# The second half of the tokens enters the up projection without its norm; the 1/rms is multiplied onto its gate and value rows

## The chip, the cores and the metric

The kernel runs on one core of a Trainium2 chip. The metric is the device time of one execution in microseconds (us). Five engines work side by side, each on its own queue of instructions in order: TensorE (PE, matrix products; its weight loads are shown as PEld), VectorE (DVE), ScalarE (ACT), GpSimd (POOL) and SyncE (SP), whose queue issues the DMA transfers here.

## The reference

One step of a hybrid decoder layer for 1024 prompt tokens and 8 single tokens of a second group, 1032 in all, in fp32. The part that matters:

```python
def rmsnorm(x, w):
    xf = x.astype(jnp.float32)
    y = xf * lax.rsqrt(jnp.mean(xf * xf, axis=-1, keepdims=True) + EPS)
    return (y * w.astype(jnp.float32)).astype(x.dtype)
...
    x = x + jnp.concatenate([o_a, y], axis=-1) @ w['w_out']

    h = rmsnorm(x, w['norm2_w'])
    gate, val = jnp.split(h @ w['w_up'], 2, axis=-1)
    gate, buf_f_new = causal_dwconv(gate, buf_f, w['ffn_conv_w'], w['ffn_conv_b'])
    x = x + (jax.nn.silu(gate) * val) @ w['w_down']
```

Ahead of it stand the input projection, a gated linear recurrence and a state-space mixer (the two that `o_a` and `y` come from), behind it a final norm. The model width is 1024, the MLP width 2816. The norm's factor 1/rms is one number for each token, so it may be multiplied onto h's inputs or onto the rows of gate and value that come out.

## The kernel before

Tokens run along the free axis, channels along the 128 partitions. An fp32 product is built from three matmuls on numbers split into a high part (`wh`, `uh`, an ACT cast) and a low part (`wl`, `ul`, a DVE subtraction): high by high, high by low, low by high.

**Out projection** (`out_job`, L1015 to L1046). Its last jobs, o4.0.hf to o4.6.hf, finish the residual rows `xh[hf][m]` (shown as x) of one half hf of the tokens: a product of 12 matmuls into a bank `mm`, then DVE adds it to x (L1040, the eviction). `final` (L1048) then sends the row to DRAM (`x1_d`), squares it on ACT (L1055, `n2sq`) and adds the square to the running sum `n2r` on POOL (L1056; the tensor is `rst` in the code).

**Norm** (`set_norm`, L1111). For a quarter of the tokens (258) PE multiplies `n2r` by a matrix of ones into a bank `n2ms`, which sums over the channels; `rstd_of` (L635) makes 1/rms of it: ACT L637, then DVE L638 to L640. The bank has the tag "nx", of which there is one (`NBANK = {"mx": 4, "nx": 1}`, L37). The first of the DVE operations, L638, still reads the bank.

**Operands of the up projection** (`set_of(i)`, L1120). The 1032 tokens form two instances, i = 0 and 1, of 516 tokens each. Of each instance's rows, four blocks are made (two halves of the channels by two quarters of the tokens), and the 2x2 block product is computed in seven products (p1 to p7) in place of eight. `norm` multiplies x by the norm's weight and by 1/rms on DVE (L1133, 8 operations an instance); `comb` makes the sums of blocks `sm` (L1151, DVE or POOL); `put` splits an operand into `uh` (ACT L1143) and `ul` (DVE L1144).

**Weights.** There are 22 weight tiles j. `up_load(j)` fetches gate and value columns (`ws`) and makes four sums of weight blocks on POOL (L1208, `wt`); `up_split(j, n)` splits two products' weights at a time (ACT L1227, DVE L1228).

**Products** (`Up`, L1236 to L1285). A product has 12 matmuls. p1, p7 and p3 go to one of three banks (`ua`), the others to one of four (`ub`). Each is evicted by the method of its name: p1 and p5 by ACT copies, p6 L1254, p7 L1262 (with two POOL subtractions L1263 and L1264), p2 L1270, p4 L1278 to L1282 and p3 L1285 by DVE. The rows of the gate go to `fext`, those of the value to `val`; `last` holds the last ten gate tokens. `up_close` runs the width-3 convolution (DVE L334 among it) and SiLU, multiplies (L1301) and stores.

**Order of the work.** PE's order is the program's own (L1317 to L1334); one `tick` is one matmul, `after(n, work)` runs a piece of code n ticks later, `spread(pieces, n)` one piece every n ticks. The other engines' instructions are ordered by a scheduler on top of that. At weight tile 0 all seven products of instance 0 come first and then all of instance 1 (`FIRST`); from tile 1 on the two instances alternate (`ORDER`). Instance 0's operands are made while the out projection of the second half still runs; instance 1's while PE works through instance 0 at tile 0. After the 22 tiles the down projection follows (`down`, bank `dn`, evicted by DVE L1387, weights split at L184 of `wload`).

Of the kernel before, what the change touches and what calls it, by code (L numbers as in the profile page):

```python
# [12 lines left out]
ALU = mybir.AluOpType  # L13
# [5 lines left out]
T = 1024  # L19
# [31 lines left out]
def hybrid_layer(  # L51
# [963 lines left out]
    def out_job(r0, m, halves=(0, 1), last=False):  # L1015
        def load():
            w = wload(w_out[0, r0 * P:(r0 + 4) * P, m * P:(m + 2) * P], 4, 2 * P)
            return w, [residual_load(m + i) for i in range(2)] if r0 == 8 else None

        def run(loads):  # L1020
            w, res = loads
            if r0 not in mixes:
                mixes[r0] = mix_load(r0)
            hi, lo = mixes[r0]
            if res:
                for hf in range(2):
                    xpair[hf][m // 2] = tl("big", "x1")[:, :NT].rearrange("p (i t) -> p i t", i=2)
                    for i in range(2):
                        xh[hf][m + i] = xpair[hf][m // 2][:, i, :]
            for i in range(2):  # L1030
                for hf in halves:
                    for c in range(2):
                        cs, ts_ = slice(c * QW, (c + 1) * QW), slice((2 * hf + c) * QW, (2 * hf + c + 1) * QW)
                        ps = psmm.tile([P, 512], F32, tag="mm", name=nm("mm"))[:, :QW]
                        yield from steps(w, i * P, (i + 1) * P, hi, lo, ts_, ps)
                        x_ = xh[hf][m + i][:, cs]
                        if res:
                            A.copy(x_, ps)
                        else:
                            V.tensor_tensor(x_, x_, ps, op=ALU.add)  # L1040
                        if last:
                            final(m + i, x_, ts_)
                        yield True
                if res:
                    spread(residual([xh[hf][m + i] for hf in range(2)], *res[i]), 8)
        job(f"o{r0}.{m}" + (f".{halves[0]}" if len(halves) == 1 else ""), load, run)  # L1046

    def final(m, x_, ts_):  # L1048

        SP.dma_start(x1_d[m][:, ts_], x_)  # L1050
        if m == 0:
            A.activation(rst[:, ts_], x_, AF.Square)
        else:
            sq = tl("us", "n2sq")
            A.activation(sq, x_, AF.Square)  # L1055
            G.tensor_tensor(rst[:, ts_], rst[:, ts_], sq, op=ALU.add)  # L1056

    xpair = [[None] * 4 for _ in range(2)]

# [59 lines left out]

    def set_of(i):  # L1120

        ts_ = slice(2 * i * QW, 2 * (i + 1) * QW)
        xp = [t.rearrange("p i (c t) -> p i c t", c=2) for t in xpair[i]]

# [30 lines left out]
            return [t[:, 0:2], t[:, 2:4]]  # L1155

        s_ = []
        yield from norm(0)
        if i:
            yield from put("p1", a1, "hT")  # L1160
        yield from norm(1)
        yield from put("p2", a2, "big")
        if i == 0:
            yield from put("p4", b2, "e")
        yield from comb(s_, V, b1, b2, ALU.subtract)
        yield from comb(s_, V, two(s_[0]), a1, ALU.subtract)
        yield from comb(s_, G, a1, b1, ALU.subtract)
        yield from comb(s_, G, two(s_[1]), a2, ALU.add)
        if i == 0:
            while "o0.6.1" not in done:  # L1170
                yield
            yield from put("p1", a1, "hT")
        else:
            yield from put("p4", b2, "big")
        yield from put("p6", [s_[1]], "hT")
        if i == 0:
            up_load(0)
        yield from put("p5", [s_[0]], "hT")
        if i == 0:
            up_split(0, 0)  # L1180
            yield
        yield from put("p7", [s_[2]], "hT")
        if i == 0:
            up_split(0, 1)
            yield
        yield from put("p3", [s_[3]], "big")

    ORDER = ("p1", "p6", "p5", "p7", "p2", "p4", "p3")

# [41 lines left out]
    class Up:  # L1231
# [40 lines left out]
        def p4(self, ps):  # L1272
# [4 lines left out]
            n = e - c.start  # L1277
            V.tensor_tensor(self.ext[:, 2 + c.start:2 + e], self.u3[:, :n], ps[:, :n], op=ALU.add)  # L1278
            if n < QW:
                dreg = self.ext[:, 2 + T:2 + T + 24].rearrange("p (b r) -> p b r", r=3)  # L1280
                V.tensor_tensor(dreg[:, :, 2:3], self.u3[:, n:].unsqueeze(2), ps[:, n:].unsqueeze(2), op=ALU.add)
                V.tensor_tensor(last10[:, self.j, :], self.u3[:, QW - 10:], ps[:, QW - 10:], op=ALU.add)  # L1282

        def p3(self, ps):
            V.tensor_tensor(self.val[:, self.at(0)], self.u2, ps, op=ALU.add)  # L1285

    def up_open(j):
        ext, val = tl("x5", "fext"), tl("x5", "val")
# [15 lines left out]
    def ups(j, seq):  # L1304

        us_ = up_open(j)
        for n, (name, i) in enumerate(seq):
            yield from us_[i].mul(name)
            if n == 2 and j + 1 < FT:
                up_load(j + 1)  # L1310
            if n in (5, 9, 13) and j + 1 < FT:
                up_split(j + 1, (5, 9, 13).index(n))
            if n == 1 and j:
                up_split(j, 3)
        up_close(j, us_[0])
# [1 line left out]
    with tc.manual_schedule(engines={mybir.EngineType.PE}):  # L1317
# [6 lines left out]
            tick()  # L1324
        up_split(0, 2)
        up_split(0, 3)
        after(20, lambda: set_norm(1, 0))
        after(29, lambda: set_norm(1, 1))
        after(33, lambda: spread(set_of(1), 2))
        for _ in ups(0, [(name, i) for i in range(2) for name in FIRST]):  # L1330
            tick()
        for j in range(1, FT):
# [124 lines left out]
```

## Time and profile before

| | us |
|---|---|
| median of 3 runs (lowest to highest) | 1781.82 (1781.15 to 1788.02) |
| the profiled execution | 1782.61 |
| its span, first to last instruction | 1780.9 |
| busy: PE, DVE, ACT, POOL | 1725.4, 1119.3, 817.5, 405.3 |
| granted TensorE clock, mean | 0.991 |

A row of a timeline reads: start, length, engine, line, operation, output<-inputs, shapes, how often in a row; in brackets how long the engine had been idle before it and which instruction released it. A row of windows gives the stretch, its length, then the busy time of PE, PEld, DVE, ACT and POOL in it with the number of instructions, the granted clock, the busy share of the DMA engines and GB/s. Matmul lengths overlap, so PE's pace is read from the distance of starts, or from the busy time of a stretch over its matmuls.

### The profile page before, as it was taken

The page shows a single profiled execution, that of the slowest core. Times are in us where ns is not written, and L with a number is a line of the kernel's source. Part 1 is how long each engine was busy: PE and PEld are TensorE (multiplying, and loading weights), DVE is VectorE, ACT ScalarE, POOL GpSimd, SP SyncE. Part 2 cuts the span into 40 slices and gives each one's busy share as a digit, 9 for nine tenths or more (in the row PEclk, how much of TensorE's full clock was granted, in tenths as well). Part 3 has the DMA queues.
Part 4 walks back from the last instruction along what each step waited for, and adds up shares of the span by engine and source line. Part 5 has one row for each costly group of instructions (what it writes and reads, how often), then busy time and mean ns, then how long its engine had stood idle before and what let it go on. Part 6 is the DMA issues. An engine that isn't in the chain of part 4 may idle for free. (4 is left out here: it accounts for less than half of the span.)

```text
span 1780.9 us, 38506 instructions
## 1 busy us (share of the span) xinstructions
PE 1725.4 (97%) x16143; PEld 1675.6 (94%) x16143; DVE 1119.3 (63%) x2011; ACT 817.5 (46%) x1464; POOL 405.3 (23%) x415
## 2 busy tenths in 40 slices
PE   7999899999999999999999978999999999999998
PEld 6998799999999999999899978999999999999997
DVE  6667966575564565458645768666666666445545
ACT  7677688455554454545333435334333344111114
POOL 2113331220110111011000364554445542000001
PEclk9999999999999999999999998999999999999999
DMA  4144634642221222234334432222222225422212
GB/s 154 39 126 126 189 106 132 184 137 98 87 66 51 86 73 78 58 109 155 101 108 133 135 90 72 72 72 78 82 91 72 72 84 203 152 81 90 97 61 96
DMA packets 218019, 182.34 MB, mean 102 GB/s; under 512 B 13388, under 2 KB 195158, under 8 KB 217830
## 3 DMA queue, kind: packets, MB, share of 16 engines
q1 hardware_dynamic: 217558, 179.80, 32.3%
q8 instruction: 126, 2.06, 0.5%
q14 instruction: 47, 0.39, 0.1%
q0 software_dynamic: 288, 0.10, 0.0%
HBM read 141.53 MB, written 38.52 MB: 101 GB/s over the span
## 5 line engine op out<-in xcount | busy, mean ns | idle before, releaser
L93 PE MATMUL mm<-hh,wh 128*128 128x344 f32 x1248 | 405.3, 325 | 0.3 <-issue 0.2
L93 PE MATMUL mm<-hl,wh 128*128 128x344 f32 x1248 | 404.5, 324 | 0.0
L93 PE MATMUL mm<-hh,wl 128*128 128x344 f32 x1248 | 402.0, 322 | 0.0
L93 PEld LDWEIGHTS mm<-hh,wh 128*128 128x128 f32 x1248 | 235.0, 189 | 3.9 <-issue 2.6
L93 PEld LDWEIGHTS mm<-hl,wh 128*128 128x128 f32 x1248 | 235.2, 189 | 2.4 <-issue 0.9
L93 PEld LDWEIGHTS mm<-hh,wl 128*128 128x128 f32 x1248 | 235.3, 189 | 2.2 <-issue 1.5
L183 ACT CAST wh<-ws 128x1024 fp32r<-128x1024 f32 x96 | 100.5, 1047 | 242.8 <-PE dn L93 135.3
L93 PE MATMUL ub<-ul,wh 128*128 128x258 f32 x704 | 200.4, 285 | 4.3 <-DVE ul L1144 4.3
L93 PE MATMUL ub<-uh,wh 128*128 128x258 f32 x704 | 200.3, 285 | 2.0 <-ACT uh L1143 2.0
L93 PE MATMUL ub<-uh,wl 128*128 128x258 f32 x704 | 200.2, 284 | 0.0
L93 PE MATMUL dn<-ah,wh 128*128 128x256 f32 (+1 forms) x640 | 181.1, 283 | 1.2 <-DVE x L1387 1.2
L93 PE MATMUL dn<-al,wh 128*128 128x256 f32 (+1 forms) x640 | 180.6, 282 | 0.0
L93 PE MATMUL dn<-ah,wl 128*128 128x256 f32 (+1 forms) x640 | 180.2, 282 | 0.0
L184 DVE TENSOR_TENSOR wl<-ws,wh 128x1024 fp32r<-128x1024 f32 x96 | 126.4, 1317 | 72.4 <-ACT wh L183 71.4
L93 PE MATMUL mm<-mh,wh 128*128 128x258 f32 x512 | 147.7, 288 | 11.2 <-DVE x L1040 8.3
L93 PE MATMUL ua<-ul,wh 128*128 128x258 f32 x528 | 149.4, 283 | 0.9 <-DVE ul L1144 0.9
L93 PE MATMUL ua<-uh,wh 128*128 128x258 f32 x528 | 149.2, 283 | 0.0
L93 PE MATMUL ua<-uh,wl 128*128 128x258 f32 x528 | 148.4, 281 | 0.0
L93 PE MATMUL mm<-ml,wh 128*128 128x258 f32 x512 | 145.8, 285 | 0.7 <-DVE ml L999 0.7
L93 PE MATMUL mm<-mh,wl 128*128 128x258 f32 x512 | 145.9, 285 | 0.0
L93 PEld LDWEIGHTS ub<-ul,wh 128*128 128x128 f32 x704 | 134.5, 191 | 5.0 <-DVE ul L1144 5.0
L93 PEld LDWEIGHTS ub<-uh,wh 128*128 128x128 f32 x704 | 134.0, 190 | 2.5 <-ACT uh L1143 2.5
(347 smaller groups left out, 3942.8 us busy)
## 6 DMA issues: line engine op xcount, KB each, us to landing
ws<-in_w_in_dram SPq DMA_DIRECT2D x52, 512.0 KB
ws<-in_w_up_dram SPq DMA_DIRECT2D x44, 512.0 KB
ws<-in_w_out_dram SPq DMA_DIRECT2D x24, 512.0 KB
act_d<-val SPq DMA_DIRECT2D x22, 516.0 KB
al<-act_d SPq DMA_DIRECT2D x22, 516.0 KB
ws<-in_w_down_dram SPq DMA_DIRECT2D x22, 512.0 KB
ml<-mix_d SPq DMA_DIRECT2D x48, 172.0 KB
csb<-cs_d SPq DMA_DIRECT2D x32, 256.0 KB
```

What stands on the lines that cost most here:

```text
L93: PE.matmul(out, lhsT, rhs, start=start, stop=stop)
L183: A.copy(wh[:, :n], ws[:, :n])
L184: V.tensor_tensor(wl[:, :n], ws[:, :n], wh[:, :n].bitcast(F32), op=ALU.subtract)
```

## The change

Instance 1 is no longer normed before its products. `weigh(m)` multiplies a row by the norm's weight alone, on ACT, 28 matmuls after the row's last product of the out projection; the eight operations L1133 of instance 1 are gone. `set_of(1)` starts 4 ticks into tile 0, was 33, and advances every 4 ticks, was 2. Both token sums of instance 1 stand together at tick 93, that is 9 matmuls into instance 1's first product; they were at ticks 20 and 29. For each weight tile, 1/rms is multiplied onto the gate rows of instance 1 (DVE, 128x508 and 128x8, after p4) and onto its value rows (POOL, 128x516, after p3); `last` becomes two small POOL copies. The weights of tile 0 are split later (the second piece 76 ticks after the first), and those of tile 1 are loaded and split later within tile 0.

```diff
@@ -1040,6 +1040,8 @@
                             V.tensor_tensor(x_, x_, ps, op=ALU.add)
                         if last:
                             final(m + i, x_, ts_)
+                            if hf and c:
+                                after(28, lambda m=m + i: weigh(m))
                         yield True
                 if res:
                     spread(residual([xh[hf][m + i] for hf in range(2)], *res[i]), 8)
@@ -1054,6 +1056,13 @@
             sq = tl("us", "n2sq")
             A.activation(sq, x_, AF.Square)
             G.tensor_tensor(rst[:, ts_], rst[:, ts_], sq, op=ALU.add)
+
+    weighed = set()
+
+    def weigh(m):
+
+        A.activation(xh[1][m], xh[1][m], AF.Copy, scale=col("n2", m))
+        weighed.add(m)
 
     xpair = [[None] * 4 for _ in range(2)]
 
@@ -1119,6 +1128,7 @@
 
     def set_of(i):
 
+
         ts_ = slice(2 * i * QW, 2 * (i + 1) * QW)
         xp = [t.rearrange("p i (c t) -> p i c t", c=2) for t in xpair[i]]
 
@@ -1155,35 +1165,40 @@
             return [t[:, 0:2], t[:, 2:4]]
 
         s_ = []
-        yield from norm(0)
-        if i:
-            yield from put("p1", a1, "hT")
-        yield from norm(1)
-        yield from put("p2", a2, "big")
         if i == 0:
+            yield from norm(0)
+            yield from norm(1)
+            yield from put("p2", a2, "big")
             yield from put("p4", b2, "e")
-        yield from comb(s_, V, b1, b2, ALU.subtract)
-        yield from comb(s_, V, two(s_[0]), a1, ALU.subtract)
-        yield from comb(s_, G, a1, b1, ALU.subtract)
-        yield from comb(s_, G, two(s_[1]), a2, ALU.add)
-        if i == 0:
+            yield from comb(s_, V, b1, b2, ALU.subtract)
+            yield from comb(s_, V, two(s_[0]), a1, ALU.subtract)
+            yield from comb(s_, G, a1, b1, ALU.subtract)
+            yield from comb(s_, G, two(s_[1]), a2, ALU.add)
             while "o0.6.1" not in done:
                 yield
             yield from put("p1", a1, "hT")
+            yield from put("p6", [s_[1]], "hT")
+            up_load(0)
+            yield from put("p5", [s_[0]], "hT")
+            yield from put("p7", [s_[2]], "hT")
+            yield from put("p3", [s_[3]], "big")
+            up_split(0, 0)
+            after(76, lambda: up_split(0, 1))
         else:
+            d_ = []
+            yield from comb(d_, G, a1, b1, ALU.subtract)
+            yield from put("p1", a1, "hT")
+            while len(weighed) < KT:
+                yield
+            yield from put("p2", a2, "big")
+            yield from comb(s_, V, b1, b2, ALU.subtract)
+            yield from comb(s_, V, two(s_[0]), a1, ALU.subtract)
+            yield from comb(s_, G, two(s_[1]), a2, ALU.add)
             yield from put("p4", b2, "big")
-        yield from put("p6", [s_[1]], "hT")
-        if i == 0:
-            up_load(0)
-        yield from put("p5", [s_[0]], "hT")
-        if i == 0:
-            up_split(0, 0)
-            yield
-        yield from put("p7", [s_[2]], "hT")
-        if i == 0:
-            up_split(0, 1)
-            yield
-        yield from put("p3", [s_[3]], "big")
+            yield from put("p6", [s_[1]], "hT")
+            yield from put("p5", [s_[0]], "hT")
+            yield from put("p7", d_, "hT")
+            yield from put("p3", [s_[2]], "big")
 
     ORDER = ("p1", "p6", "p5", "p7", "p2", "p4", "p3")
 
@@ -1277,12 +1292,20 @@
             n = e - c.start
             V.tensor_tensor(self.ext[:, 2 + c.start:2 + e], self.u3[:, :n], ps[:, :n], op=ALU.add)
             if n < QW:
-                dreg = self.ext[:, 2 + T:2 + T + 24].rearrange("p (b r) -> p b r", r=3)
-                V.tensor_tensor(dreg[:, :, 2:3], self.u3[:, n:].unsqueeze(2), ps[:, n:].unsqueeze(2), op=ALU.add)
-                V.tensor_tensor(last10[:, self.j, :], self.u3[:, QW - 10:], ps[:, QW - 10:], op=ALU.add)
+
+                ext, t0 = self.ext, self.at(0).start
+                dnew = ext[:, 2 + T:2 + T + 24].rearrange("p (b r) -> p b r", r=3)[:, :, 2:3]
+                V.tensor_tensor(dnew, self.u3[:, n:].unsqueeze(2), ps[:, n:].unsqueeze(2), op=ALU.add)
+                V.tensor_tensor(ext[:, 2 + t0:2 + T], ext[:, 2 + t0:2 + T], rst[:, t0:T], op=ALU.mult)
+                V.tensor_tensor(dnew, dnew, rst[:, T:NT].unsqueeze(2), op=ALU.mult)
+                G.tensor_copy(last10[:, self.j, 0:2], ext[:, T:T + 2])
+                G.tensor_copy(last10[:, self.j, 2:10].unsqueeze(2), dnew)
 
         def p3(self, ps):
             V.tensor_tensor(self.val[:, self.at(0)], self.u2, ps, op=ALU.add)
+            if self.i:
+                t0 = self.at(0).start
+                G.tensor_tensor(self.val[:, t0:NT], self.val[:, t0:NT], rst[:, t0:NT], op=ALU.mult)
 
     def up_open(j):
         ext, val = tl("x5", "fext"), tl("x5", "val")
@@ -1306,10 +1329,11 @@
         us_ = up_open(j)
         for n, (name, i) in enumerate(seq):
             yield from us_[i].mul(name)
-            if n == 2 and j + 1 < FT:
+            if n == (2 if j else 5) and j + 1 < FT:
                 up_load(j + 1)
-            if n in (5, 9, 13) and j + 1 < FT:
-                up_split(j + 1, (5, 9, 13).index(n))
+            at_ = (5, 9, 13) if j else (9, 11, 13)
+            if n in at_ and j + 1 < FT:
+                up_split(j + 1, at_.index(n))
             if n == 1 and j:
                 up_split(j, 3)
         up_close(j, us_[0])
@@ -1324,9 +1348,8 @@
             tick()
         up_split(0, 2)
         up_split(0, 3)
-        after(20, lambda: set_norm(1, 0))
-        after(29, lambda: set_norm(1, 1))
-        after(33, lambda: spread(set_of(1), 2))
+        after(4, lambda: spread(set_of(1), 4))
+        after(93, lambda: (set_norm(1, 0), set_norm(1, 1)))
         for _ in ups(0, [(name, i) for i in range(2) for name in FIRST]):
             tick()
         for j in range(1, FT):
```

Three places show how the instructions stand now. (Line numbers of the changed kernel are higher: L1144 became L1154, L1151 L1161, L1228 L1243, L1254 L1269, L1262 L1277, L1270 L1285, L1278 L1293, L1285 L1305.)

PE at the token sums `n2ms` of instance 1, before: the first stands inside p2 of instance 0 (`ub_1488`), the second in p4 (`ub_1491`), ten matmuls later.

```order
L93 MATMUL ub_1488_12430<-ul_1404_11922,wh_1446_12166 128x258
L93 MATMUL n2ms_1489_12439<-n2r_125_804,ones_550 128x258
L93 MATMUL ub_1488_12430<-uh_1403_11921,wl_1447_12167 128x258
L93 MATMUL ub_1488_12430<-uh_1403_11921,wh_1446_12166 128x258
L93 MATMUL ub_1488_12430<-ul_1404_11922,wh_1446_12166 128x258
L93 MATMUL ub_1488_12430<-uh_1403_11921,wl_1447_12167 128x258
L93 MATMUL ub_1491_12451<-uh_1407_11949,wh_1453_12205 128x258
L93 MATMUL ub_1491_12451<-ul_1408_11950,wh_1453_12205 128x258
L93 MATMUL ub_1491_12451<-uh_1407_11949,wl_1454_12206 128x258
L93 MATMUL ub_1491_12451<-uh_1407_11949,wh_1453_12205 128x258
L93 MATMUL ub_1491_12451<-ul_1408_11950,wh_1453_12205 128x258
L93 MATMUL n2ms_1492_12457<-n2r_125_804,ones_550 128x258
```

The same of the changed kernel: both stand next to each other inside p1 of instance 1 (`ua_1521`).

```order
L93 MATMUL ua_1521_12585<-uh_1488_12438,wh_1453_12204 128x258
L93 MATMUL ua_1521_12585<-ul_1489_12439,wh_1453_12204 128x258
L93 MATMUL ua_1521_12585<-uh_1488_12438,wl_1454_12205 128x258
L93 MATMUL n2ms_1522_12595<-n2r_125_804,ones_550 128x258
L93 MATMUL n2ms_1524_12602<-n2r_125_804,ones_550 128x258
L93 MATMUL ua_1521_12585<-uh_1488_12438,wh_1453_12204 128x258
L93 MATMUL ua_1521_12585<-ul_1489_12439,wh_1453_12204 128x258
L93 MATMUL ua_1521_12585<-uh_1488_12438,wl_1454_12205 128x258
```

The two sums share one bank, and between them there was a product's worth of other matmuls; now there is none.

DVE around the operations that read these sums, before: `nt_1490` (L638, reads the first sum) stands right behind the last weight split of tile 0 (`wl_1483`) and ahead of instance 1's norm (L1133).

```order
L1228 TENSOR_TENSOR wl_1483_12408<-ws_1434_12132,wh_1482_12407 128x512
L638 SCALAR_TENSOR_TENSOR nt_1490_12441<-n2ms_1489_12439,n2r_125_804 128x258
L1270 TENSOR_TENSOR fext_1484_12411<-us_1487_12428,ub_1488_12430 128x258
L639 SCALAR_TENSOR_TENSOR nt_1490_12441<-nt_1490_12441,n2r_125_804 128x258
L640 SCALAR_TENSOR_TENSOR n2r_125_804<-nt_1490_12441,n2r_125_804 128x258
L638 SCALAR_TENSOR_TENSOR nt_1493_12459<-n2ms_1492_12457,n2r_125_804 128x258
L639 SCALAR_TENSOR_TENSOR nt_1493_12459<-nt_1493_12459,n2r_125_804 128x258
L640 SCALAR_TENSOR_TENSOR n2r_125_804<-nt_1493_12459,n2r_125_804 128x258
L1133 SCALAR_TENSOR_TENSOR x1_1129_9594<-x1_1129_9594,vcol_99,n2r_125_804 128x516 x2
L1133 SCALAR_TENSOR_TENSOR x1_1151_9891<-x1_1151_9891,vcol_99,n2r_125_804 128x516 x2
```

DVE of the changed kernel, the rows ahead of `nt_1523`, which reads the first sum: instance 1's sums (`sm`), low parts (`ul`) and the evictions of instance 0's products. Ahead of these rows, from the last eviction of the out projection on, stand `wl_1483`, `ul_1489`, `fext_1484` (of p2), `sm_1495` and `ul_1494`, one instruction each.

```order
L1161 TENSOR_TENSOR sm_1497_12492<-sm_1495_12480,x1_1151_9891 128x516
L1269 TENSOR_TENSOR us_1498_12499<-us_1490_12442,ub_1496_12482 128x258
L1154 TENSOR_TENSOR ul_1502_12518<-x1_1239_10571,uh_1501_12517 128x516
L1154 TENSOR_TENSOR ul_1502_12518<-x1_1257_10716,uh_1501_12517 128x516
L1154 TENSOR_TENSOR ul_1506_12535<-sm_1497_12492,uh_1505_12534 128x1032
L1154 TENSOR_TENSOR ul_1520_12577<-sm_1500_12506,uh_1519_12576 128x1032
L1154 TENSOR_TENSOR ul_1508_12543<-sm_1495_12480,uh_1507_12542 128x1032
L1277 TENSOR_TENSOR us_1509_12546<-us_1498_12499,ua_1504_12523 128x258
L1154 TENSOR_TENSOR ul_1518_12569<-sm_1487_12427,uh_1517_12568 128x1032
L1293 TENSOR_TENSOR fext_1484_12417<-us_1509_12546,ub_1492_12460 128x258
L1305 TENSOR_TENSOR val_1485_12418<-us_1498_12499,ua_1516_12563 128x258
L638 SCALAR_TENSOR_TENSOR nt_1523_12597<-n2ms_1522_12595,n2r_125_804 128x258
```

L638 moved from ahead of instance 1's operands to behind them all.

DVE in the out projection of the second half, before: the split of the weight sums `wt_1438` and `wt_1436` stands behind the eviction of `mm_1449`.

```order
L1040 TENSOR_TENSOR x1_1151_9891<-x1_1151_9891,mm_1445_12159 128x258
L1144 TENSOR_TENSOR ul_1451_12188<-sm_1418_12028,uh_1450_12187 128x1032
L1040 TENSOR_TENSOR x1_1151_9891<-x1_1151_9891,mm_1449_12183 128x258
L1228 TENSOR_TENSOR wl_1454_12206<-wt_1438_12140,wh_1453_12205 128x512
L1228 TENSOR_TENSOR wl_1454_12206<-wt_1436_12136,wh_1453_12205 128x512
L1144 TENSOR_TENSOR ul_1457_12222<-sm_1424_12058,uh_1456_12221 128x1032
L1040 TENSOR_TENSOR x1_1151_9891<-x1_1151_9891,mm_1455_12211 128x258
L1040 TENSOR_TENSOR x1_1151_9891<-x1_1151_9891,mm_1459_12233 128x258
L184 TENSOR_TENSOR wl_1463_12253<-ws_1461_12251,wh_1462_12252 128x1024
```

The same of the changed kernel: the first splits now read plain weights (`ws_1433`), and that of `wt_1438` stands behind the evictions of `mm_1455` and `mm_1457`.

```order
L1040 TENSOR_TENSOR x1_1151_9891<-x1_1151_9891,mm_1445_12159 128x258
L1040 TENSOR_TENSOR x1_1151_9891<-x1_1151_9891,mm_1449_12182 128x258
L1243 TENSOR_TENSOR wl_1454_12205<-ws_1433_12130,wh_1453_12204 128x512 x2
L1040 TENSOR_TENSOR x1_1151_9891<-x1_1151_9891,mm_1455_12210 128x258
L1040 TENSOR_TENSOR x1_1151_9891<-x1_1151_9891,mm_1457_12229 128x258
L1243 TENSOR_TENSOR wl_1472_12331<-wt_1438_12140,wh_1471_12330 128x512
L184 TENSOR_TENSOR wl_1461_12249<-ws_1459_12247,wh_1460_12248 128x1024
L1040 TENSOR_TENSOR x1_1239_10571<-x1_1239_10571,mm_1462_12253 128x258
```

The split that waits for POOL's sums moved behind two more evictions.

## The prediction

> **What bounds the kernel now.** I read the page first, then the waits of the tensor engine (PE), then the timelines at the two places where it waits, and last the steady part of the up projection.
>
> ```profile
> span 1780.9 us, 38506 instructions
> PE 1725.4 (97%) x16143; PEld 1675.6 (94%) x16143; DVE 1119.3 (63%) x2011; ACT 817.5 (46%) x1464; POOL 405.3 (23%) x415
> ```
>
> PE is busy for 97% of the span and executes the same products after the change, so only its pauses, its clock, and new pauses can move the time. A window over one weight tile of the up projection (columns: length, then busy time of PE, PEld, DVE, ACT, POOL, granted clock) and a piece of the chain of work that ended last:
>
> ```profile
> 1250.00:1270.15 20.15, 20.15 (x171) 20.15 (x169) 13.38 (x23) 7.76 (x14) 9.41 (x10) 1.00 0.25 80
> 1263.25 5.75 PE ua L93 x48
> ```
>
> PE never pauses there; 48 matmuls take 5.75 us, 0.1197 each, so a product of 12 takes 1.437. What the change can win lies between the out projection and the steady part. PE's waits from 970 to 1100 us (total, times, longest):
>
> ```profile
> PE mm L93 <- DVE x L1040: 8.0, 4, 6.8
> PE ub L93 <- DVE ul L1144: 4.3, 3, 2.8
> PE ub L93 <- ACT uh L1143: 2.0, 2, 1.5
> PE n2ms L93 <- POOL n2r L1056: 1.0, 1, 1.0
> PE ua L93 <- DVE ul L1144: 0.9, 1, 0.9
> ```
>
> **Place A** is the first row, a single pause of 6.76 us in the out projection. Rows of PE, DVE, ACT and POOL (start, length, and in brackets the idle time before):
>
> ```profile
> 1039.04 0.58 PE L93 MATMUL mm<-mh,wh 128*128 128x258 f32 x1 [6.76 <-DVE x L1040]
> 1035.76 1.74 DVE L1228 TENSOR_TENSOR wl<-wt,wh 128x512 fp32r<-128x512 f32 x2 [5.29 <-ACT wh L1227]
> 1035.11 0.62 ACT L1227 CAST wh<-wt 128x512 fp32r<-128x512 f32 x1 [1.50 <-POOL wt L1208]
> 1033.82 1.26 POOL L1208 TENSOR_TENSOR wt<-wt,ws 128x512 f32<-128x512 f32 x1
> 1035.04 0.73 POOL L1056 TENSOR_TENSOR n2r<-n2r,n2sq 128x258 f32<-128x258 f32 x1
> 1037.43 1.22 DVE L1144 TENSOR_TENSOR ul<-sm,uh 128x1032 fp32r<-128x1032 f32 x1
> 1038.57 0.74 DVE L1040 TENSOR_TENSOR x<-x,mm 128x258 f32<-128x258 f32 x2
> 1034.00:1036.00 2.00, 0.00 (x0) 0.00 (x0) 0.24 (x1) 0.89 (x3) 1.77 (x2) 0.89 0.00 0
> ```
>
> DVE stands still with the evictions L1040 queued behind a weight split whose cast waits for POOL's sums L1208. **Place B** is instance 0 and 1 at weight tile 0, from the first `ua` at 1050.88 to the next tile at 1084.66:
>
> ```profile
> 1050.88 0.28 PE L93 MATMUL ua<-uh,wh 128*128 128x258 f32 x1
> 1084.66 0.28 PE L93 MATMUL ua<-uh,wh 128*128 128x258 f32 x1
> 1056.27 0.67 PE L93 MATMUL n2ms<-n2r,ones 128*128 128x258 f32 x2
> 1075.58 0.58 PE L93 MATMUL ub<-ul,wh 128*128 128x258 f32 x1 [2.80 <-DVE ul L1144]
> 1058.88 3.60 DVE L1133 SCALAR_TENSOR_TENSOR x<-x,vcol,n2r 128x516 f32<-128x516 f32 x4
> 1060.00:1070.00 10.00, 7.23 (x52) 6.41 (x51) 10.00 (x15) 2.77 (x5) 3.04 (x2) 0.98 0.00 1
> 1070.00:1080.00 10.00, 5.67 (x26) 5.08 (x25) 10.00 (x11) 6.37 (x9) 5.91 (x4) 0.50 0.00 0
> ```
>
> It lasts 33.78 us; its 168 matmuls at 0.1197 are 20.1. The other 13.7 split into operand waits (4.3 + 2.0 + 0.9 = 7.2, rows of the waits), the two token sums with their wait (1.0 plus twice about 0.65, so 2.3) and the remainder, 4.2, which is the half clock: in the second window 26 matmuls take 5.67, 0.218 each instead of 0.12. DVE is full (10.00 of 10.00) and is the cause: instance 1's norm may only begin at 1058.88.
>
> In these rows the clock falls after a stretch of thin PE work and returns some us later. The Trainium skill ("TensorE: Matmul & The Clock Gate", Part 1, "What's actually happening") says the clock is gated by activity over free-running windows of 3.41 us; the granted 0.50 over 1070 to 1080 agrees. By that rule a new pause longer than a window would bring half clock again, as I charge below from the rows.
>
> **The change at A.** The order of DVE now puts two more evictions ahead of the split that needs POOL's sums (in front of it only a split of plain weights). So PE does two more products, 2 x 1.437 = 2.87, before it meets the same wait. That wait does not end earlier: the sums are the same POOL work, one `n2r` addition (0.73) now stands among them, so the last sum ends near 1035.8, its cast (0.62) near 1036.4, then DVE has a split (0.7), one 1.2 operation and the eviction: PE goes on at about 1039.1, as before. Gain 2.87, less a second, shorter pause with its own half clock: between 0 and 1.2. I take **2.2** (1.7 to 2.8).
>
> **The change at B, what goes.** Eight DVE operations L1133 leave (3.60 for four, 7.2 us); eight ACT multiplications take their place, earlier, and wait for no token sum. Instance 1's operands then start at tick 4 rather than after the norm. All 7.2 of operand wait goes, and the 1.0 of the first token sum, whose POOL additions are long over at tick 93. ACT has room: busy 2.77 and 6.37 in the two windows; if a multiplication must wait for the store of its row, casts queue behind it, which is part of the spread below.
>
> **The change at B, what comes.** The two token sums now stand back to back on PE, and both use the one PSUM bank of tag "nx". The second can start only when DVE L638 has read the first. That L638 stands in DVE's queue behind all of instance 1's operands. Prices of what is queued there:
>
> ```profile
> L1144 DVE TENSOR_TENSOR ul<-x,uh x12: 681/684/1636, 1010.1 to 1075.4; 128x516 fp32r<-128x516 f32 x12
> L1144 DVE TENSOR_TENSOR ul<-sm,uh x8: 1219/1222/1768, 1023.0 to 1080.0; 128x1032 fp32r<-128x1032 f32 x8
> 1261.80 0.74 POOL L1264 TENSOR_TENSOR us<-us,us 128x258 f32<-128x258 f32 x1
> 1259.95 1.18 POOL L1264 TENSOR_TENSOR us<-us,us 128x258 f32<-128x258 f32 x1
> 1062.56 1.49 POOL L1151 TENSOR_TENSOR sm<-x 128x516 f32<-128x516 f32 x1 [0.63 <-DVE x L1133]
> 1063.01 1.59 DVE L1133 SCALAR_TENSOR_TENSOR x<-x,vcol,n2r 128x516 f32<-128x516 f32 x1
> 1062.41 0.68 DVE L1144 TENSOR_TENSOR ul<-x,uh 128x516 fp32r<-128x516 f32 x1
> 1265.03 0.42 DVE L1285 TENSOR_TENSOR val<-us,ua 128x258 f32<-128x258 f32 x1
> ```
>
> Call S the start of the first `ua`. From the last eviction at S + 0.4 DVE has seven operations of 0.68, four of 1.22 and five evictions of 0.42 ahead of L638: 4.8 + 4.9 + 2.1 = 11.8, about 10.8 with the overlap of 0.07 at each start that the rows show. Two waits come on top: the sum that needs the last row's multiplication, whose store can only leave after S + 0.5 (about 1.5), and the last eviction, for POOL's two subtractions after DVE L1262 (0.74 to 1.18 each, of which some 1.3 is uncovered). L638 ends near S + 14.2. PE arrives after 93 matmuls and one token sum, S + 11.4. **The new pause is 2.8 us at the least.** A DVE operation with two SBUF inputs that meets a POOL operation takes longer: 1.59 at 1063.01 beside POOL's 1.49 begun at 1062.56, against 0.68 alone. Four to five of the queued ones can meet POOL's sums and subtractions, at 0.7 to 0.9 each: up to 3.6 more, so 6.4 at the upper end. I take **5.2**, nearer to the upper end because that stage of before is full of such meetings (the maxima 1636 and 1768 ns in the two rows).
>
> A pause of 5.2 costs clock too: at A a pause of 6.8 was followed by some 15 slow matmuls (1.4 us); at B 4.2 was lost. I charge 2.0. The token sums themselves cost 1.0. So B becomes 20.1 + 1.0 + 5.2 + 2.0 = 28.3 instead of 33.8: gain **5.5**.
>
> **The steady part.** For each of the 22 weight tiles DVE gets a 128x508 multiplication with both inputs in SBUF (0.68 by the row of 128x516) and one of 128x8 (0.16 by the row of `last` below), and loses `last`; POOL gets a 128x516 multiplication (1.49 by its row, at most) and two tiny copies. DVE rises from 13.4 to 14.1, with a meeting to 14.9, POOL to about 11.3, of 20.15: neither becomes the bound by its sum. What decides is whether an eviction comes late:
>
> ```profile
> 1263.69 0.16 DVE L1282 TENSOR_TENSOR last<-us,ub 128x10 f32<-128x10 f32 x1
> 1506.84 1.21 DVE L184 TENSOR_TENSOR wl<-ws,wh 128x1024 fp32r<-128x1024 f32 x1
> 1515.31 0.39 PE L93 MATMUL dn<-ah,wh 128*128 128x256 f32 x1 [0.89 <-DVE x L1387]
> 1505.00:1515.00 10.00, 9.12 (x73) 8.52 (x71) 10.00 (x15) 6.25 (x7) 0.00 (x0) 1.00 0.83 323
> ```
>
> The eviction behind the multiplication is that of p3 of instance 0: it ends at 1265.45, and its bank (of three) is needed by the fourth product of the chain's piece, 1263.25 + 3 x 1.437 = 1267.56. That is 2.1 us of cover against 0.7 to 1.6 added: cost 0 (bounds 0 and, if the cover is used up, rival 2).
>
> The Trainium skill ("SBUF — State Buffer", "Who interferes with whom") speaks against this part: a VectorE instruction with two SBUF inputs and a GpSimd one that reads SBUF exclude each other for the whole instruction. The rows at 1063.01 and 1062.56 agree. By the rule every tile could lose up to 1.5 us of DVE time; by the row 0.9; either is inside the cover alone.
>
> **The end of the up projection** has no cover: DVE is full from 1505 to 1515, and the down projection's first weights (1506.84) stand right behind the added multiplication. PE waits there already. Cost **0.8** (0.5 to 1.5).
>
> **Sum**, against the profiled execution of 1782.61 us (span 1780.9 and 1.7 around it; the median of the runs is 1781.82, 0.8 lower): 1782.61 - 2.2 - 5.5 + 0.8 = 1775.7.
>
> **Rivals.**
> 1. *Little contention.* The pause at the second token sum is 2.8 with 1.0 of slow clock: B 24.9, gain 8.9; A 2.8; end 0.5: about 1771.4. For it: POOL has few operations in that stretch (3.04 and 5.91 of 10). Against: each one so far met DVE.
> 2. *The multiplication per tile delays PE, slower than before.* If meetings of DVE and POOL push the eviction of p3 more than 2.1 us, every tile loses the excess. At 0.8 over: 22 x 0.8 = 17.6, so about 1793. For it: two splits of 0.7 stand between. Against: 0.7 + 0.9 is under 2.1, and DVE has 5 us free per tile.
> 3. *The new wait eats the gain.* If the last row's store comes late or ACT's casts queue behind it, the pause is 8.5 with 3.5 of slow clock: B 33.1, gain 0.7; A 1.7; end 1.0: about 1781.2.
>
> **How the numbers follow.** Forecast (1773 to 1779.5) 0.50, rival 1 0.24, rival 3 (1779.5 to 1783) 0.14, rival 2 0.10, anything else 0.02. The range 1770.5 to 1782.0 takes in the first three nearly whole. A difference of 0.5%, 8.9 us, is about what a measurement of this kernel can tell from no change: faster than 1772.9 is rival 1, 0.24; slower than 1790.7 is rival 2, 0.10; between them 0.66.
>
> **What would show it.** In the changed profile: one PE wait of `n2ms` for DVE L638 of 3 to 6 us; no wait for L1144 behind S; the pause at A two products later and half as long or a little more, with resumption near 1039; 20.15 us per tile unchanged. A tile longer than 20.3, or a wait of `ua` for DVE L1285, would make it wrong, as would a pause at `n2ms` of under 2 or over 8.

## The result: no difference, where 7 us less were forecast

The changed kernel takes 1784.82 us (median of 14 runs, 1780.36 to 1787.37); the kernel before took 1784.93 beside it (14 runs, 1781.15 to 1789.09). The ratio is 0.9998, with a 95% interval of 0.9986 to 1.0009. The forecast was 1775.7, and its range ended at 1782.0. Of the 9.1 us between forecast and median, 2.3 are the starting point: the forecast started from a profiled execution of 1782.61, and the larger set of runs of the same kernel has its median at 1784.93. The other 6.8 are the change itself, which was to win 6.9 and won 0.1.

The head of the page of the changed kernel (profiled execution 1784.84 us, granted clock 0.992):

```profile
span 1782.0 us, 38562 instructions
PE 1723.3 (97%) x16143; PEld 1674.7 (94%) x16143; DVE 1132.6 (64%) x2025; ACT 823.7 (46%) x1472; POOL 484.4 (27%) x481
```

PE executes the same 16143 matmuls. POOL is busy 79 us longer, DVE 13. The waits of PE from 970 to 1100 us, the table that had five rows before:

```profile
PE n2ms L93 <- DVE nt L638: 8.7, 1, 8.7
PE mm L93 <- DVE x L1040: 6.1, 5, 3.7
```

All waits for operands (L1143, L1144, in all 7.2 us) are gone, as forecast, and the pause at place A is 3.7 instead of 6.8. One new pause takes their place: 8.68 us at the second token sum, where 5.2 had been put. The rows of PE, first at A, then from S (the first `ua`) to the sums:

```profile
1040.16 0.39 PE L93 MATMUL mm<-mh,wh 128*128 128x258 f32 x1 [3.67 <-DVE x L1040]
1049.00 0.28 PE L93 MATMUL ua<-uh,wh 128*128 128x258 f32 x1
1069.42 1.20 PE L93 MATMUL n2ms<-n2r,ones 128*128 128x258 f32 x2 [8.68 <-DVE nt L638]
```

PE came to the second sum at 1069.42 - 8.68 = 1060.74, that is S + 11.7 (forecast S + 11.4). The other side of the wait, DVE, was late. DVE's rows from the end of the out projection to L638:

```profile
1047.39 1.77 DVE L1161 TENSOR_TENSOR sm<-x,x 128x516 f32<-128x516 f32 x1 [0.67 <-ACT x L1064]
1049.19 1.67 DVE L1161 TENSOR_TENSOR sm<-sm,x 128x516 f32<-128x516 f32 x1
1050.78 0.41 DVE L1040 TENSOR_TENSOR x<-x,mm 128x258 f32<-128x258 f32 x1
1051.11 2.50 DVE L1154 TENSOR_TENSOR ul<-x,uh 128x516 fp32r<-128x516 f32 x2
1053.54 0.41 DVE L1040 TENSOR_TENSOR x<-x,mm 128x258 f32<-128x258 f32 x1
...
1059.12 0.68 DVE L1161 TENSOR_TENSOR sm<-sm,x 128x516 f32<-128x516 f32 x1
...
1068.52 0.42 DVE L1305 TENSOR_TENSOR val<-us,ua 128x258 f32<-128x258 f32 x1 [0.97 <-POOL us L1279]
1068.86 0.42 DVE L638 SCALAR_TENSOR_TENSOR nt<-n2ms,n2r 128x258 f32<-128x258 f32 x1
```

The last eviction of the out projection (the second L1040) starts at 1053.54, which is S + 4.5, and not at S + 0.4. In the kernel before, with S at 1050.88, it starts at S + 0.2:

```profile
1051.08 0.42 DVE L1040 TENSOR_TENSOR x<-x,mm 128x258 f32<-128x258 f32 x1 [1.12 <-PE mm L93]
```

In the changed kernel four operations of instance 1 stand ahead of it, and they are slow: the sums of 1.77 and 1.67 are of the same kind and shape as the one that takes 0.68 at 1059.12. POOL's rows beside them show what they meet, weight sums L1223 and the additions of squares L1058 without a gap:

```profile
1048.56 1.75 POOL L1223 TENSOR_TENSOR wt<-ws,ws 128x512 f32<-128x512 f32 x1
1050.26 1.09 POOL L1058 TENSOR_TENSOR n2r<-n2r,n2sq 128x258 f32<-128x258 f32 x1
...
1053.02 3.40 POOL L1058 TENSOR_TENSOR n2r<-n2r,n2sq 128x258 f32<-128x258 f32 x3
```

PE's clock through the pause and behind it (length, then busy time of PE, PEld, DVE, ACT, POOL, granted clock), and the steady tile at the end:

```profile
1060.70:1064.00 3.30, 0.05 (x1) 0.00 (x0) 3.30 (x4) 2.41 (x5) 0.44 (x1) 1.00 0.00 0
1064.00:1069.40 5.40, 0.00 (x0) 0.01 (x1) 4.39 (x8) 1.39 (x3) 2.25 (x2) 0.61 0.00 0
1069.40:1075.40 6.00, 5.97 (x26) 5.81 (x27) 3.50 (x8) 1.99 (x4) 0.00 (x0) 0.50 0.00 0
1250.00:1270.15 20.15, 20.15 (x170) 20.15 (x169) 13.65 (x24) 7.86 (x14) 13.10 (x13) 1.00 0.25 81
```

The clock falls within the pause and stays at 0.50 for 6.0 us after it. A tile still takes 20.15 us, with DVE at 13.65 and POOL at 13.10 of it.

To add up pieces of several traces, four points are used: M, the `mm` matmul near 1004 us that waits 0.36 for an eviction, up to which the kernels below run the same program; S; T1, the first matmul of weight tile 1; and F, the first group of transposes `fin` on the chain of work that ended last. The tail runs from F to the last `fin` on that chain.

| us | M | M to S | S to T1 | T1 to F | tail | M to end of tail |
|---|---|---|---|---|---|---|
| before | 1004.25 | 46.63 | 33.77 | 662.30 | 24.39 | 767.09 |
| changed | 1004.38 | 44.62 | 32.62 | 663.10 | 27.96 | 768.30 |

The changed kernel wins 2.0 in the out projection and 1.15 in tile 0, and gives back 0.8 up to F and 3.6 in the tail. The chain of the tail shows where the last comes in:

```profile
1744.72 1.75 PE fin L1435 x16
...
1751.61 4.36 DMA out_dram<-ot
...
1772.68 0.45 PE fin L1435 x4
```

In this trace the chain passes through an output transfer of 4.36 us; in that of before it passes through none.

### The profile page after: what moved, and what is told of

Its sections match the earlier page's. It is cut to its first block, busy times and chain, and to the rows that moved or that the text cites. A ratio compares the mean times of both kernels' runs of the same rounds, so it can differ in the third digit from the quotient of the medians.

```text
span 1782.0 us, 38562 instructions
## 1 busy us (share of the span) xinstructions
PE 1723.3 (97%) x16143; PEld 1674.7 (94%) x16143; DVE 1132.6 (64%) x2025; ACT 823.7 (46%) x1472; POOL 484.4 (27%) x481
```

## The experiments

Two theories stood for the pause of 8.68. **Single bank**: it exists because the second sum needs the one bank of tag "nx", which L638 frees from the end of DVE's queue; with another bank it goes. **DVE backlog**: DVE is that late whatever the bank, and PE would meet it a few matmuls later at the bank of an eviction.

**The second sum into another bank** (e1 in the expectations below). It takes one of the four "mx" banks:

```diff
-        ps = bank("n2ms", "nx")
+        ps = bank("n2ms", "mx" if i and c else "nx")
```

> The changed kernel, but the second token sum goes to one of the four banks of the other tag, so it need not wait until DVE has read the first. Theory 'single bank' (the pause of 8.7 us is the shared bank and nothing else): PE no longer pauses at the sums, the half clock behind it goes too, weight tile 1 starts 8 to 11 us earlier than the 1081.6 of the changed kernel. Theory 'DVE backlog' (DVE is late with everything, L638 is only the first that PE meets): PE runs into the next result of DVE instead, the bank of instance 0's p4, which DVE L1293 frees at S + 18.5; as the borrowed bank shifts the turn, p2 of instance 1 waits for it, from S + 12.1: a pause of about 6.4, tile 1 about 2.5 us earlier, a time within 0.3% of the changed kernel.

Measured: 1778.58 us (8 runs), ratio to before 0.9960 (0.9942 to 0.9979); S to T1 24.27, which is 8.35 less than in the changed kernel's first trace and 6.4 less than in its second one (30.68, below). M to the end of the tail is 760.07, 7.0 less than before, as the ratio has it. PE's waits from 1040 to 1105 us:

```profile
PE mm L93 <- DVE x L1040: 3.7, 1, 3.7
PE ub L93 <- DVE fext L1293: 2.3, 1, 2.3
PE ua L93 <- DVE val L1305: 1.3, 1, 1.3
PE ub L93 <- DVE nt L638: 0.4, 1, 0.4
```

The pause is gone, and the half clock with it (granted 1.00 from 1060 to 1080). The backlog is real but small: 2.3 + 0.4 in tile 0. Single bank is the larger part of it, 6.4 to 8.4 with the clock. The row of 1.3 lies in tile 1, where DVE's rows show the multiplication L1299 ahead of the eviction that PE waits for:

```profile
1097.47 1.19 DVE L1299 TENSOR_TENSOR fext<-fext,n2r 128x508 f32<-128x508 f32 x1
1098.58 0.16 DVE L1300 TENSOR_TENSOR fext<-fext,n2r 128x8 f32<-128x8 f32 x1
1098.66 0.68 DVE L1243 TENSOR_TENSOR wl<-ws,wh 128x512 fp32r<-128x512 f32 x1
1099.26 0.41 DVE L1305 TENSOR_TENSOR val<-us,ua 128x258 f32<-128x258 f32 x1
```

**The two sums apart, one bank** (e2). 47 matmuls between them:

```diff
-        after(93, lambda: (set_norm(1, 0), set_norm(1, 1)))
+        after(93, lambda: set_norm(1, 0))
+        after(140, lambda: set_norm(1, 1))
```

> The changed kernel, but the second token sum stands at tick 140 and not at 93 beside the first. Theory 'single bank': no pause of more than 1 us is left, tile 1 starts 9 to 11 us earlier than 1081.6. Theory 'DVE backlog': p4 of instance 1 waits for the bank that DVE L1293 frees at S + 18.5, from S + 13.5 on: a pause of 5.0 in place of 8.7, with less half clock behind it, tile 1 about 4 to 5 us earlier (1077).

Measured: 1779.2 us (10 runs), ratio 0.9961 (0.9946 to 0.9975), S to T1 24.64. PE's waits over the same stretch:

```profile
PE mm L93 <- DVE x L1040: 3.7, 1, 3.7
PE ub L93 <- DVE fext L1293: 1.4, 1, 1.4
PE ua L93 <- DVE val L1305: 0.9, 1, 0.9
PE n2ms L93 <- DVE nt L638: 0.6, 1, 0.6
```

Distance does what a second bank does, and DVE's first L638 still stands 64.5 us after M. So the cost lay in asking for the bank again at once, as single bank has it.

**Why L638 was later than forecast: fewer POOL additions** (e6). Twelve of POOL's additions of squares of instance 1 are left out, so part of its token sum is missing; the order of DVE's queue stays.

```diff
-            G.tensor_tensor(rst[:, ts_], rst[:, ts_], sq, op=ALU.add)
+            if ts_.start < 2 * QW or m < 2:
+                G.tensor_tensor(rst[:, ts_], rst[:, ts_], sq, op=ALU.add)
```

> The changed kernel without POOL's additions of the squares of rows 2 to 7 for the second half of the tokens (12 POOL operations of 1.1 us; that part of the token sum is left out). Theory 'contention' (the pause of 8.7 is larger than my least one of 2.8 because DVE operations with two SBUF inputs stand behind POOL operations; 1.77 us for a sum that takes 0.68 alone): those of DVE's operations that met the additions fall back to 0.7 or 1.2 us, the pause at the second token sum shrinks to 4 to 6 us. Theory 'order' (DVE is late because sums of instance 1 stand ahead of the last two evictions and wait for ACT's multiplications and for stores): the pause stays between 8 and 9.

Measured in one profiled execution (1783.62 us): a pause of 6.19, and L638 61.4 us after M instead of 64.5. PE's wait, then DVE's rows up to the last eviction (S is 1054.41 here) and one of POOL's weight sums beside them:

```profile
PE n2ms L93 <- DVE nt L638: 6.2, 1, 6.2
```

```profile
1053.02 1.53 DVE L1162 TENSOR_TENSOR sm<-x,x 128x516 f32<-128x516 f32 x1 [0.77 <-ACT x L1065]
1054.58 1.68 DVE L1162 TENSOR_TENSOR sm<-sm,x 128x516 f32<-128x516 f32 x1
...
1056.51 1.29 DVE L1155 TENSOR_TENSOR ul<-x,uh 128x516 fp32r<-128x516 f32 x2
1057.72 0.41 DVE L1040 TENSOR_TENSOR x<-x,mm 128x258 f32<-128x258 f32 x1
```

```profile
1053.95 1.75 POOL L1224 TENSOR_TENSOR wt<-wt,ws 128x512 f32<-128x512 f32 x1
```

The two low parts take 1.29 together instead of 2.50, and meeting these additions explains 3.1 us of L638's time. The pause lies between what the two theories expected (4 to 6, 8 to 9). The eviction is still at S + 3.3, but that doesn't show the order alone: the two sums ahead of it still take 1.53 and 1.68 beside POOL's weight sums, where they take 0.68 alone. With 0.68 each the eviction would start at about S + 1.5 (an estimate from these rows). So POOL is the larger cause; that the order by itself holds DVE back is read from the rows, and no run here separates it.

**The multiplications left out** (e5). Instance 1's gate and value rows then lack 1/rms altogether:

```diff
-                V.tensor_tensor(ext[:, 2 + t0:2 + T], ext[:, 2 + t0:2 + T], rst[:, t0:T], op=ALU.mult)
-                V.tensor_tensor(dnew, dnew, rst[:, T:NT].unsqueeze(2), op=ALU.mult)
...
-                G.tensor_tensor(self.val[:, t0:NT], self.val[:, t0:NT], rst[:, t0:NT], op=ALU.mult)
```

> The changed kernel without the multiplications by 1/rms per weight tile (instance 1's gate and value rows stay un-normed, and that part of the result is left out). From the start of tile 1 to the down projection's first matmul after its two waits the changed kernel takes 431.45 us, the kernel before 430.65. If the multiplications cost only at the end of the up projection, as predicted: 430.65, each tile 20.15 in both. If they cost PE in each tile, some 0.04 a tile: the difference is spread. Rival: the small POOL copies or the changed turn of the weight loads cost it, then 431.4 stays.

Measured: 1781.0 us (10 runs), ratio to before 0.9972 (0.9956 to 0.9988); T1 to F 661.02 where the changed kernel has 663.10. The multiplications cost about 2.1 us from T1 to F. PE is not delayed in every tile: from T1 to the first matmul of the down projection it takes 423.36 us in the changed kernel, 423.08 without the multiplications and 423.09 before. Where they cost shows in PE's waits from 1490 to 1520 us, at the change to the down projection, first of the changed kernel, then without the multiplications, then of the kernel before:

```profile
PE dn L93 <- DVE x L1410: 1.9, 2, 1.0
```

```profile
PE dn L93 <- DVE wl L184: 0.4, 1, 0.4
```

```profile
PE dn L93 <- DVE x L1387: 1.2, 2, 0.9
```

Without the multiplications 1.5 of wait goes, which is most of the 2.1. Against the kernel before, with which the forecast compared, the waits of the changed kernel are 0.7 longer. The late eviction in tile 1 that the first experiment shows is not part of it: in the changed kernel PE doesn't wait there in the first trace, and 0.3 us in the second.

**The later weight splits alone** (e4), on the kernel before:

```diff
-        if i == 0:
-            up_split(0, 0)
-            yield
         yield from put("p7", [s_[2]], "hT")
-        if i == 0:
-            up_split(0, 1)
-            yield
         yield from put("p3", [s_[3]], "big")
+        if i == 0:
+            up_split(0, 0)
+            after(76, lambda: up_split(0, 1))
...
-            if n == 2 and j + 1 < FT:
+            if n == (2 if j else 5) and j + 1 < FT:
...
-            if n in (5, 9, 13) and j + 1 < FT:
-                up_split(j + 1, (5, 9, 13).index(n))
+            at_ = (5, 9, 13) if j else (9, 11, 13)
+            if n in at_ and j + 1 < FT:
+                up_split(j + 1, at_.index(n))
```

> The kernel before, with only the later splits of tile 0's weights and the later load and splits of tile 1's (part d of the change). If the order of the splits alone makes the gain in the out projection, the pause there falls from 6.8 to about 3.7 us and the first ua starts at 1049.0 as in the changed kernel (1050.9 before), and tile 1 at about 1082.8 (before 1084.7). If the gain came from the ACT multiplications or from the fewer DVE operations of the norm, it stays at 1050.9.

Measured: 1781.43 us (10 runs), ratio 0.9984 (0.9966 to 1.0002), M to S 45.62, M to T1 78.16 (before 80.40). The pause at A:

```profile
1038.01 0.58 PE L93 MATMUL mm<-mh,wh 128*128 128x258 f32 x1 [4.04 <-DVE x L1040]
```

It is down from 6.76 by this part alone, so the shorter pause at A belongs to the order of the splits. S comes 1.0 earlier than before, about half of what was expected. The rest of the change adds little to that: M to T1 is 77.24 and 76.49 in the two traces of the changed kernel.

**Both kernels once more** (e10 and e12), unchanged, for the scatter of the pieces.

> The changed kernel again, for a second trace. In the first one the down projection's output tail took 28.0 us from the first transposes to the last (24.4 in the kernel before, 25.8 in e1, e2 and e5), with a wait of 4.4 us for an output transfer on the chain. If the tail belongs to the changed program: 28 again. If it is luck of the transfers: another value, 24 to 26. The pause at the second token sum should be 8.7 again, whatever the start.

> The kernel before again, for a second trace. The point from which I measure (the first pause of the last out-projection jobs) lay between 1001.9 and 1012.1 us in the traces so far, with the same program ahead of it: I expect another value in that range. The output tail (first transposes to last): 24.4 if it belongs to the program, as in the kernel before and in e4, against 25.7 to 25.8 in six traces of kernels with the multiplications or the un-normed instance.

| us | M | M to S | S to T1 | T1 to F | tail | M to end of tail |
|---|---|---|---|---|---|---|
| before again | 1008.72 | 46.85 | 33.90 | 662.06 | 24.33 | 767.14 |
| changed again | 1012.09 | 45.81 | 30.68 | 663.37 | 25.71 | 765.57 |

PE's wait at the second sum in the second trace of the changed kernel:

```profile
1077.18 1.20 PE L93 MATMUL n2ms<-n2r,ones 128*128 128x258 f32 x2 [7.53 <-DVE nt L638]
```

L638 stands 64.5 us after M in both traces of the changed kernel and with the other bank too. It does not follow PE, so a later S makes the pause shorter one for one (8.68 with 44.62, 7.53 with 45.81), and the expectation of 8.7 whatever the start was wrong. The tail is not 28 again, so the 28.0 belongs to the first trace and not to the program. M itself moves by 7.7 us between two traces of one kernel, which is more than the change does; the sums from M to the end of the tail, -1.6 to +1.2 against before, lie within the interval of the ratio (-2.5 to +1.6 us).

**Other bank, operands later** (e8). Instance 1's operands start at tick 16, every 5. On DVE this moves the evictions L1277, L1293 and L1305 of instance 0's products ahead of one large low part each; the four operations ahead of the last L1040 stay, and it starts at S + 3.6:

```diff
-        after(4, lambda: spread(set_of(1), 4))
+        after(16, lambda: spread(set_of(1), 5))
```

> The changed kernel with the second token sum in another bank (as e1), and instance 1's operands started at tick 16 and advanced every 5 ticks; on DVE the evictions L1277 and L1293 then stand ahead of one and two of the large low parts that they stood behind. In e1 PE still lost 2.3 us to L1293 and 0.4 to L638 within tile 0, which lasted 24.3 us from the first ua. If the backlog on DVE is what is left: the wait for L1293 shrinks to about 1 us, tile 0 to about 23 us, and the time is 1 to 1.5 us under e1's. If the operands now come late instead, PE waits for L1154 and tile 0 is 24 us or more.

Measured: 1777.9 us (5 runs), ratio 0.9962 (0.9948 to 0.9977), S to T1 24.22. PE's waits in tile 0 and 1:

```profile
PE ub L93 <- DVE nt L638: 1.5, 1, 1.5
PE ua L93 <- DVE val L1305: 1.3, 1, 1.3
PE ub L93 <- DVE fext L1293: 1.1, 1, 1.1
```

Against 24.27 with the other bank alone, nothing: what L1293 gains (1.1 for 2.3), L638 loses (1.5 for 0.4), and L638 stands 64.6 us after M as ever. DVE's work is only moved.

**Other bank, value rows on DVE** (e9). The multiplication of the value rows goes from POOL to DVE:

```diff
-                G.tensor_tensor(self.val[:, t0:NT], self.val[:, t0:NT], rst[:, t0:NT], op=ALU.mult)
+                V.tensor_tensor(self.val[:, t0:NT], self.val[:, t0:NT], rst[:, t0:NT], op=ALU.mult)
```

> The kernel of e1, but the value rows of instance 1 are multiplied by 1/rms on DVE and not on POOL. In the changed kernel this POOL operation takes 2.9 us on average, and in e1 PE waits once 1.3 us for DVE L1305 in an early tile, behind POOL's weight sums. From the start of tile 1 to the down projection's first matmul after its waits e1 takes 432.8 us, the kernel before 430.7. If POOL's queue and its exclusion of DVE cost that: 431 to 431.5 here, the early wait gone. If DVE's own time is the limit: 433 or more, with waits for DVE at the end of the up projection longer than 1.0 and 0.9.

Measured: 1777.63 us (5 runs), ratio 0.9955 (0.9941 to 0.9968), below that of the changed kernel (0.9986 to 1.0009); T1 to F 663.29, 1.2 less than with the other bank alone, S to T1 23.96. The early wait for L1305 is 0.8 instead of 1.3; it was expected to go. Against the other bank alone (0.9960) the difference is inside the intervals.

**The same with one square for a row** (e11) of the second half, instead of one for each quarter (half as many additions on POOL):

```diff
+        if ts_.start >= 2 * QW:
+            if ts_.start < 3 * QW:
+                return
+            x_, ts_ = xh[1][m], slice(2 * QW, 4 * QW)
+            sq = tl("q", "n2sq") if m else None
```

> The kernel of e9 (second token sum in another bank, value rows multiplied on DVE), and the squares of the second half of the tokens are taken and added once a row (128x516) in place of once a quarter (128x258): 7 POOL additions for 14. Leaving 12 additions out (e6) brought DVE's L638 3.1 us nearer to the fixed point in the out projection. If that was POOL's exclusion of DVE, half as many, longer additions give back 1 to 2 us: tile 0 about 22.5 to 23.5 us from the first ua (e9 24.0), and the pause in the out projection changes by at most a product. The time is 1 to 2 us under e9's. If the longer additions exclude DVE as long in sum: tile 0 stays at 24.

Measured: 1778.21 us (5 runs), ratio 0.9952 (0.9939 to 0.9966): no gain over the last one. S to T1 rises to 26.77, where 22.5 to 23.5 or 24 was expected. PE's two waits in tile 0, and the clock behind the second:

```profile
1064.26 0.39 PE L93 MATMUL ub<-uh,wh 128*128 128x258 f32 x1 [0.97 <-ACT us L1278]
...
1068.70 0.39 PE L93 MATMUL ub<-uh,wh 128*128 128x258 f32 x1 [2.71 <-DVE fext L1298]
```

```profile
1066.00:1068.70 2.70, 0.00 (x1) 0.00 (x1) 2.64 (x4) 2.16 (x6) 1.36 (x1) 1.00 0.00 0
1068.70:1069.00 0.30, 0.30 (x2) 0.30 (x3) 0.00 (x0) 0.00 (x0) 0.30 (x2) 1.00 0.00 0
1069.00:1072.40 3.40, 3.40 (x19) 3.40 (x17) 2.77 (x9) 1.14 (x2) 0.60 (x1) 0.52 0.00 0
```

A new wait for ACT (L1278 here) comes ahead of that for DVE, and half clock behind both.

## Why the prediction was wrong

**Place A: the pause right, the gain short.** The pause was to be two products later and half as long; it is 3.67 for 6.76, and the splits alone do it. S came 2.0 earlier in one trace and 0.9 in the other (forecast 2.2, 1.7 to 2.8). PE was to go on at the same time as before; it goes on 35.8 us after M in both traces, where before had 34.8, so 1.0 of the 2.87 is gone there. The rest is the half clock, which the shorter pause doesn't shorten: in the first trace 16 matmuls behind it follow each other at about 0.21 us and in the second 27, against 14 and 16 behind the pause of 6.7 to 6.8 in the traces of before.

**Place B, what goes: right.** All operand waits behind S are gone, and none came in their place.

**Place B, the new wait: the mechanism was right, its start was wrong, and this is the step that failed.** The sentence was "From the last eviction at S + 0.4 DVE has seven operations of 0.68, four of 1.22 and five evictions of 0.42 ahead of L638". That eviction starts at S + 4.5 (S + 3.4 in the second trace, S + 0.2 in both traces of before and with the splits alone). The count began at a row of DVE's order and gave it a time from PE's side, when its bank is ready. It did not ask what stands ahead of it on DVE: two sums L1161, of which the first waits for an ACT multiplication (0.67), and two low parts L1154, in all 5.94 us beside POOL where they would take 2.7 alone. That is 4.1 us: 3.2 by POOL and, by the same rows, 0.9 by the order and the wait. From there to the end of L638 it took 15.7, where 13.8 and 2.4 for meetings with POOL had been put, so 0.5 less than forecast. PE came 0.3 later. The pause is 5.2 + 4.1 - 0.5 - 0.3 = 8.5, measured 8.68 and 7.53. The clock behind it cost 2.8 and 2.1 (S to T1 less 20.1 of matmuls, 1.0 of sums and the pause), forecast 2.0. So B gave 1.2 and 3.2 instead of 5.5. Rival 3 named this size of pause (8.5), but gave another reason, the late store. The wait for ACT's multiplication is 0.67 in the first trace and absent in the second, so that its number came close is luck.

The Trainium skill ("SBUF — State Buffer", "Who interferes with whom") has a VectorE instruction with two SBUF inputs and a GpSimd one that reads SBUF lock each other out. The rows agree (1.77 against 0.68, and 1.29 against 2.50 for two with additions left out). The error lay in charging it only behind the last eviction.

**The steady part: right.** A tile takes 20.15 with and without the multiplications. The mechanism of rival 2 happens at most once, in tile 1 (nothing and 0.3 us in the two traces of the changed kernel, 0.8 to 1.3 in e1, e2, e8 and e9), not in every tile.

**The end of the up projection: right.** PE waits 1.9 there and 1.2 before, so 0.7 more, for 0.8 forecast; over T1 to F the changed kernel is 0.9 and 1.2 longer than the mean of before (662.18).

**Not in the sum at all: the tail.** It is 24.3 to 24.4 in both traces of before and with the splits alone, 25.7 to 25.8 in all kernels with the rest of the change, and 28.0 in one trace of the changed kernel. It is so without the multiplications too (25.77), so these are not the cause. The order of instructions there is the same. On the chain an output transfer of about 4 us appears where before had none; why the chain runs through it was not settled and stays open.

Taken together, of the 6.8 us that the change lacks, the pause at B with its clock takes 3.3 (mean of two traces), A 0.7, the stretch to F 0.2 and the tail about 2.5.

## What to carry to other kernels

When a wait is to be timed, follow the releasing engine's queue backwards from the releasing instruction until a row whose start is known from that engine itself; a start taken from another engine's side leaves out what is queued ahead. Two uses of a bank from a ring of one, back to back, wait for their reader's place in its queue: another bank or 47 matmuls between took 6 to 8 us off the first tile here and turned no difference into 0.4%. Work moved earlier off one engine's wait lands beside other work: here beside POOL's sums and additions, where it took twice as long.

## What the runs showed of the hardware

The POOL multiplication of the value rows was priced at no more than 1.49 us; in the steady part it takes almost twice that, while DVE's own multiplication stays near its price (groups of the changed kernel from 1090 to 1490 us: busy, mean ns of one, idle before):

```profile
L1308 POOL TENSOR_TENSOR val<-val,n2r 128x516 f32<-128x516 f32 x20 | 58.1, 2903 | 44.5 <-DVE val L1305 44.5
```

```profile
L1299 DVE TENSOR_TENSOR fext<-fext,n2r 128x508 f32<-128x508 f32 x20 | 14.5, 725 | 0.0
```

With one square for a row the granted clock fell to 0.52 for 3.4 us behind pauses of 0.97 and 2.71 us with twelve matmuls between them; with the other bank a pause of 2.3 left it at 1.00. The Trainium skill ("TensorE: Matmul & The Clock Gate", Part 1, "HAM oscillation — how this bites in real kernels") gives the rule as "no PE-idle gaps >~3.4µs"; the trace with 2.71 does not fit it, since there the clock fell with no gap of that length. What share of a window must be idle is not shown by these runs.
